# One-hot rows by scalar-operand instructions, a re-laid gate table, and GpSimd without elementwise work in the expert stages of a hybrid decoder layer

## The chip, the cores and the metric

The kernel runs on one core of a Trainium2 chip. The metric is the device time of the whole program in microseconds (us). The core has a matmul engine (PE, with its weight loads as PEld), a vector engine (DVE), a scalar engine (ACT), GpSimd (POOL) and a queue processor (SP) that issues most DMA transfers; sixteen DMA engines move the data. Each engine runs its own instructions in the order in which they stand.

## What is computed

A decoder layer over 512 positions of width 1024: RMS norm, one input projection, three groups of attention heads, an output projection with a residual, and then an expert retrieval. All of it is float32. The change lies in the last part:

```python
qry = (h @ w_q).reshape(B, S, PEER_HEADS, PEER_DKEY)
s1 = jnp.einsum('bshd,hkd->bshk', qry[..., :half], sub1)
s2 = jnp.einsum('bshd,hkd->bshk', qry[..., half:], sub2)
v1, i1 = lax.top_k(s1, PEER_TOPK)
v2, i2 = lax.top_k(s2, PEER_TOPK)
...
top_s, pos = lax.top_k(cand, PEER_TOPK)
expert = jnp.take_along_axis(cand_idx, pos, axis=-1)
gate = jax.nn.softmax(top_s, axis=-1)
...
def step(args):
    x_c, e_c, g_c = args
    a = jnp.einsum('cd,ced->ce', x_c, u[e_c])
    w = jax.nn.gelu(a, approximate=False) * g_c
    return jnp.einsum('ce,ced->cd', w, v[e_c])
```

Each position picks 8 x 16 = 128 of 16,384 experts (tables u and v, 64 MB each) and adds their gated outputs.

## The kernel before, in words

The 512 positions are four chunks of 128. Chunk 0 (GC) takes its experts by **gather**: for each of its 128 slots, GpSimd fetches one row of u per position by an indirect DMA (L475) and the vector engine forms the dot product (L482); then the same with v, where the vector engine adds even slots into one accumulator `ga` (L493) and GpSimd adds odd slots into a second one (L491) after the scalar engine has scaled the row (L490). Rows lie in four buffers, so GpSimd waits with a fetch until a row has been used.

The other three chunks (DC, TD = 384 positions) are computed **dense**: all 128 blocks of 128 experts are multiplied, and a gate table that is zero for experts not chosen picks out what counts. An fp32 product is made of three matmuls (L95 to L97) over a rounded part "hi" (scalar engine, L86) and a remainder "lo" (L87: a subtraction, 128x1024 for a block of u or v). `u_parts` (L514) loads a block of u and splits it; its remainder is GpSimd's. `a_block` (L521) multiplies it with the positions and applies the gelu (L527).

The stages as they lie in time:

- to about 300 us: attention and output projection, not touched;
- 315 to 562 us: expert queries, top-16 selections and `route` (L413), which turns the selections into expert numbers and gates, with the first blocks of u beside it. Some of `route`'s products (L442) stay on GpSimd in both kernels;
- 562 to 909 us, the **one-hot stage**: for each chunk `route` gives a tile `iT` with two key numbers and the gate of every slot. For four positions at a time the vector engine compares the key numbers with a ramp `iota` (L591, L592: 128x512 each), the second result is multiplied with the gate (half the times on the vector engine, L595; half on the scalar engine, L597), and PE multiplies the two (L600): 128 x 128 gates of one position. The scalar engine writes them to a tile `stage` (L601), and each 32 positions go out to HBM as a quarter of 2 MB (L602; `stage` has two buffers). Meanwhile the first 64 blocks of u run (NSP), and their results go to HBM (L607);
- 909 us to the end, the **table stage**: `w_block` (L628) runs 128 times. It reads its part of the gate table (L637, for four blocks at a time), loads a block of v (L641) and splits it (L86, L87), multiplies gelu and gate (L645), splits that, and issues 18 matmuls of 512 columns. 64 of these blocks also compute their u half here.

A scheduler sets the order of the instructions on each engine from its own forecast of the times, so an edit in one place moves instructions in others.

## Time and profile before

| | us |
|---|---|
| median of three runs | 1754.59 |
| lowest and highest | 1750.6, 1756.23 |
| span of the profiled execution, first to last instruction | 1749.3 |
| PE busy in it | 1592.6 |
| DVE busy | 1442.9 |
| POOL busy | 968.3 |

The profiled execution has no time of its own beside its span; the median lies 5.3 us above that span. The share of busy time is an average over stages that wait for different engines, so the profile is read by stage: which engine has no idle time there, and how long its instructions take against the shortest of the same form.

### The profile page before, as it was taken

The page shows a single profiled execution, that of the slowest core. Times are in us where ns is not written, and L with a number is a line of the kernel's source. Part 1 is how long each engine was busy: PE and PEld are TensorE (multiplying, and loading weights), DVE is VectorE, ACT ScalarE, POOL GpSimd, SP SyncE. Part 2 cuts the span into 40 slices and gives each one's busy share as a digit, 9 for nine tenths or more (in the row PEclk, how much of TensorE's full clock was granted, in tenths as well). Part 3 has the DMA queues.
Part 4 walks back from the last instruction along what each step waited for, and adds up shares of the span by engine and source line. Part 5 has one row for each costly group of instructions (what it writes and reads, how often), then busy time and mean ns, then how long its engine had stood idle before and what let it go on. Part 6 is the DMA issues. An engine that isn't in the chain of part 4 may idle for free.

```text
span 1749.3 us, 23459 instructions
## 1 busy us (share of the span) xinstructions
PE 1592.6 (91%) x8045; PEld 1397.1 (80%) x8045; DVE 1442.9 (82%) x2552; ACT 787.2 (45%) x1287; POOL 968.3 (55%) x531
## 2 busy tenths in 40 slices
PE   7999989997686878878999999999999999899997
PEld 6886667997686777778998888888888888788885
DVE  6556745899999999979956877877889978889896
ACT  6345633332332555667843333334444443444442
POOL 4220013363776675734465544456778867788774
PEclk9999999998888989889999999999999999999998
DMA  8302034132566566557699999998999999898894
GB/s 322 106 25 103 1 121 144 49 125 90 181 212 198 182 218 216 176 222 280 231 315 325 279 318 288 315 286 279 291 287 278 317 290 275 255 309 276 288 277 171
DMA packets 317463, 390.08 MB, mean 223 GB/s; under 512 B 214944, under 2 KB 240544, under 8 KB 314656
## 3 DMA queue, kind: packets, MB, share of 16 engines
q1 hardware_dynamic: 280480, 254.36, 46.0%
q0 software_dynamic: 36864, 134.23, 21.6%
q8 instruction: 63, 1.03, 0.2%
q14 instruction: 56, 0.46, 0.1%
HBM read 346.57 MB, written 41.94 MB: 222 GB/s over the span
## 4 chain that ended last, share of the span: by engine, by line
PE 49%; DVE 36%; issue 5%; DMA 5%; ACT 2%; SPq 2%; POOL 2%; DVEq 0%; ACTq 0%; POOLq 0%
PE s L96 7%; PE s L97 7%; PE s L95 6%; PE t L95 5%; PE t L97 5%; PE t L96 5%; DVE row L482 5%; DVE o L591 5%; DVE o L592 4%; PE o L96 3%; PE o L97 3%; PE o L95 3%; DVE eq L440 2%; PE o L330 2%; DVE og L595 2%
## 5 line engine op out<-in xcount | busy, mean ns | idle before, releaser
L87 POOL TENSOR_TENSOR yT<-flat,yT 128x1024 fp32r<-128x1024 f32 x128 | 346.6, 2709 | 216.4 <-ACT yT L86 208.7
L95 PE MATMUL t<-hT,yT 128*128 128x384 f32 x1024 | 351.4, 343 | 26.1 <-ACT ag L527 26.1
L97 PE MATMUL t<-hT,yT 128*128 128x384 f32 x1024 | 351.4, 343 | 2.4 <-POOL yT L87 2.4
L96 PE MATMUL t<-hT,yT 128*128 128x384 f32 x1024 | 350.3, 342 | 0.0
L87 DVE TENSOR_TENSOR yT<-vr,yT 128x1024 fp32r<-128x1024 f32 x128 | 209.5, 1637 | 54.7 <-ACT yT L86 51.5
L475 POOL DMA_INDIRECT row<-u,exp_g x128 | 161.7, 1263 | 124.0 <-DVE row L482 88.3
L95 PEld LDWEIGHTS t<-hT,yT 128*128 128x128 f32 x1024 | 197.0, 192 | 32.5 <-ACT ag L527 27.3
L96 PE MATMUL s<-yT,ws 128*128 128x512 f32 x512 | 206.7, 405 | 11.1 <-DVE yT L87 10.8
L482 DVE SCALAR_TENSOR_TENSOR row<-row,hg 128x1024 f32<-128x1024 f32 x128 | 189.2, 1482 | 24.0 <-DMA row<-u,exp_g 24.0
L97 PE MATMUL s<-yT,ws 128*128 128x512 f32 x512 | 201.4, 402 | 4.2 <-DVE ws L87 4.2
L475 POOL DMA_INDIRECT row<-v,exp_g x128 | 156.1, 1219 | 84.9 <-DVE ga L493 49.6
L86 ACT ACTIVATE ws<-w 128x384 fp32r<-128x384 f32 x128 | 67.1, 524 | 299.4 <-DVE w L645 118.7
L97 PEld LDWEIGHTS t<-hT,yT 128*128 128x128 f32 x1024 | 196.8, 192 | 5.7 <-POOL yT L87 3.0
L96 PEld LDWEIGHTS t<-hT,yT 128*128 128x128 f32 x1024 | 196.8, 192 | 4.5
L86 ACT ACTIVATE yT<-flat 128x1024 fp32r<-128x1024 f32 x128 | 135.4, 1058 | 144.2 <-issue 53.6
L491 POOL TENSOR_TENSOR ga<-ga,row 128x1024 f32<-128x1024 f32 x64 | 164.1, 2564 | 26.1 <-ACT row L490 25.4
L95 PE MATMUL s<-yT,ws 128*128 128x512 f32 x512 | 165.1, 399 | 7.8 <-ACT ws L86 7.8
L86 ACT ACTIVATE yT<-vr 128x1024 fp32r<-128x1024 f32 x128 | 134.2, 1048 | 57.4 <-DMA vr<-v 44.0
L600 PE MATMUL s<-og,o 128*128 128x128 f32 x768 | 109.7, 296 | 54.8 <-DVE og L595 38.4
L600 PEld LDWEIGHTS s<-og,o 128*128 128x128 f32 x768 | 103.1, 208 | 63.4 <-issue 39.6
L87 DVE TENSOR_TENSOR ws<-w,ws 128x384 fp32r<-128x384 f32 x128 | 119.8, 937 | 41.0 <-ACT ws L86 36.2
L493 DVE SCALAR_TENSOR_TENSOR ga<-row,gw,ga 128x1024 f32<-128x1024 f32 x64 | 143.2, 2238 | 6.6 <-DMA row<-v,exp_g 6.4
(268 smaller groups left out, 3249.2 us busy)
## 6 DMA issues: line engine op xcount, KB each, us to landing
flat<-uT SPq DMA_DIRECT2D x128, 512.0 KB
vr<-v SPq DMA_DIRECT2D x128, 512.0 KB
gd<-stage SPq DMA_DIRECT2D x12, 2048.0 KB
gt<-gd SPq DMA_DIRECT2D x384, 64.0 KB
ad<-ag SPq DMA_DIRECT2D x64, 192.0 KB
agr<-ad SPq DMA_DIRECT2D x64, 192.0 KB
wraw<-w_in SPq DMA_DIRECT2D x8, 1024.0 KB
flat<-w_q SPq DMA_DIRECT2D x16, 512.0 KB
```

The lines of the kernel that those rows point to most:

```text
L86: A.activation(hi, src, AF.Copy)
L87: return (e_lo or V).tensor_sub(lo, src, hi.bitcast(F32))
L95: T.matmul(o, ah, bh, start=start, stop=False)
L96: T.matmul(o, ah, bl, start=False, stop=False)
L97: T.matmul(o, al, bh, start=False, stop=stop)
L475: G.indirect_dma_start(out=row, out_offset=None, in_=table, in_offset=bass.IndirectOffsetOnAxis(ap=exp_g[:, s_:s_ + 1], axis=0))
L482: V.scalar_tensor_tensor(row, row, 1.0, hg, ALU.mult, ALU.mult, accum_out=av[:, s_:s_ + 1])
L491: G.tensor_add(ga[1], ga[1], row)
L493: V.scalar_tensor_tensor(ga[0], row, gw[:, s_:s_ + 1], ga[0], ALU.mult, ALU.add)
L591: V.tensor_tensor(o1, bc(iT[:, 0, :]), ib, ALU.is_equal)
L592: V.tensor_tensor(o2, bc(iT[:, 1, :]), ib, ALU.is_equal)
L600: T.matmul(gp[:, j, :], o1[:, j, :], og[:, j, :], start=True, stop=True)
```

## The change

- **One-hot**: per position, two instructions with a scalar operand for each partition. The first compares `iota` with the first key number; the second compares with the second key number and multiplies with the gate in the same instruction. 96 + 96 + 48 vector instructions of 128x512 and 192 scalar-engine instructions become 768 vector instructions of 128x128.
- **Gate table**: it is laid out in HBM by block, position row and position (`gd[NK, P, TD]`). A quarter is written in runs of 32 floats (128 bytes) instead of one run of 16 KB for each partition; a read of four blocks is one transfer with runs of 384 floats instead of twelve transfers that fill runs of 32 floats.
- **GpSimd**: the remainder of every block of u is computed on the vector engine, and all 128 slots of v are added by the vector engine into one accumulator. GpSimd keeps the indirect fetches and 20 products of `route`.

```diff
-    gd = [[dram.tile([P, NK, GT], F32, name=f"gd{c}_{q}") for q in range(P // GT)] for c in range(len(DC))]
+    gd = dram.tile([NK, P, TD], F32, name="gd")
...
             row = gather(v, s_)
-            if s_ % 2:
-                A.activation(row, row, AF.Copy, scale=gw[:, s_:s_ + 1])
-                G.tensor_add(ga[1], ga[1], row)
-            else:
-                V.scalar_tensor_tensor(ga[0], row, gw[:, s_:s_ + 1], ga[0], ALU.mult, ALU.add)
+            V.scalar_tensor_tensor(ga[0], row, gw[:, s_:s_ + 1], ga[0], ALU.mult, ALU.add)
...
-                    V.tensor_tensor(o1, bc(iT[:, 0, :]), ib, ALU.is_equal)
-                    V.tensor_tensor(o2, bc(iT[:, 1, :]), ib, ALU.is_equal)
-                    og = oh.tile([P, 4, NK], F32, tag="og", name="og", bufs=3)
-                    if OGD[t4 // 4 % len(OGD)] == "V":
-                        V.tensor_mul(og, o2, bc(iT[:, 2, :]))
-                    for j in range(0 if OGD[t4 // 4 % len(OGD)] == "V" else 4):
-                        A.activation(og[:, j, :], o2[:, j, :], AF.Copy, scale=iT[:, 2, t0 + j:t0 + j + 1])
+                    for j in range(4):
+                        i1, i2, gate = (iT[:, i, t0 + j:t0 + j + 1] for i in range(3))
+                        V.tensor_scalar(o1[:, j, :], iota, i1, None, ALU.is_equal)
+                        V.tensor_scalar(o2[:, j, :], iota, i2, gate, ALU.is_equal, ALU.mult)
...
-                        T.matmul(gp[:, j, :], o1[:, j, :], og[:, j, :], start=True, stop=True)
+                        T.matmul(gp[:, j, :], o1[:, j, :], o2[:, j, :], start=True, stop=True)
...
-                DMA.dma_start(gd[ci_][q], stage)
+                DMA.dma_start(gd[:, :, ci_ * P + q * GT:ci_ * P + (q + 1) * GT].rearrange("b p t -> p b t"), stage)
...
-                u_parts(loaded, loaded % 4, dict(G=G, V=V)[UL[loaded % len(UL)]])
+                u_parts(loaded, loaded % 4, V)
...
-                gt = vb.tile([P, NB, len(DC), P], F32, tag="gt", name="gt")
-                for ci_ in range(len(DC)):
-                    for q in range(P // GT):
-                        DMA.dma_start(gt[:, :, ci_, q * GT:(q + 1) * GT], gd[ci_][q][:, g0:g0 + NB, :])
+                gt = vb.tile([P, NB, TD], F32, tag="gt", name="gt")
+                DMA.dma_start(gt, gd[g0:g0 + NB].rearrange("b p t -> p b t"))
...
-                        u_parts(a, a % 2, G)
+                        u_parts(a, a % 2, V)
```

The edits move instructions on every engine. Three places show it (line numbers of the changed kernel are some 2 to 16 lower than those of the kernel before).

GpSimd near the end of the table stage, before: `yT<-flat` is the remainder of a block of u, `ga` the second accumulator, `row<-v` an indirect fetch.

```order
L475 DMA row<-v,exp_g 128x1024 x2
L491 TENSOR_TENSOR ga_1428<-ga_1428,row 128x1024
L87 TENSOR_TENSOR yT_1453<-flat,yT_1452 128x1024
L475 DMA row<-v,exp_g 128x1024 x2
L491 TENSOR_TENSOR ga_1428<-ga_1428,row 128x1024
L475 DMA row<-v,exp_g 128x1024 x2
L491 TENSOR_TENSOR ga_1428<-ga_1428,row 128x1024
```

GpSimd from the one-hot stage to the end, in the changed kernel:

```order
L440 TENSOR_TENSOR eq<-eq,ci 128x800 x2
L473 DMA row<-u,exp_g 128x1024 x7
L440 TENSOR_TENSOR eq<-eq,ci 128x800 x4
L473 DMA row<-u,exp_g 128x1024 x71
L473 DMA row<-v,exp_g 128x1024 x128
```

Between its fetches GpSimd has only `route`'s products left, and none after the 57th fetch of u.

The vector engine in the one-hot stage, before: the two comparisons and the gate product stand mixed with the dot products of the gathered rows.

```order
L592 TENSOR_TENSOR o_5220<-iT,iota 128x512
L482 SCALAR_TENSOR_TENSOR row,av<-row,hg 128x1024
L592 TENSOR_TENSOR o_5235<-iT,iota 128x512
L591 TENSOR_TENSOR o_5207<-iT,iota 128x512
L595 TENSOR_TENSOR og<-o_5208,iT 128x512
```

The same engine at the start of the one-hot stage in the changed kernel:

```order
L584 TENSOR_SCALAR o_4640<-iota,iT 128x128
L585 TENSOR_SCALAR o_4641<-iota,iT 128x128
L440 TENSOR_TENSOR eq<-eq,ci 128x800 x2
L445 TENSOR_TENSOR pe<-wv,wm 128x128
L85 TENSOR_TENSOR yT_1442<-flat,yT_1441 128x1024
L480 SCALAR_TENSOR_TENSOR row,av<-row,hg 128x1024
L85 TENSOR_TENSOR yT_1442<-flat,yT_1441 128x1024
L480 SCALAR_TENSOR_TENSOR row,av<-row,hg 128x1024
L85 TENSOR_TENSOR yT_1442<-flat,yT_1441 128x1024
L480 SCALAR_TENSOR_TENSOR row,av<-row,hg 128x1024
L584 TENSOR_SCALAR o_4656<-iota,iT 128x128
L585 TENSOR_SCALAR o_4657<-iota,iT 128x128
```

The remainders of u (L85) now stand in the vector engine's queue, each beside a dot product; the comparisons stand in runs, later for several quarters on end. Before the first `w` of the table stage the queue holds 71 remainders of u and 75 dot products, against 0 and 65 before.

The DMA queue of SP in the one-hot stage of the changed kernel: `gd<-stage` is a quarter of the gate table, `flat<-uT` a block of u, `ad<-ag` the result of a block.

```order
L590 DMA gd<-stage 128x128x32 x3
L510 DMA flat<-uT 128x1024 x3
L595 DMA ad_117<-ag 128x384
L595 DMA ad_118<-ag 128x384
L595 DMA ad_119<-ag 128x384
L510 DMA flat<-uT 128x1024
L595 DMA ad_120<-ag 128x384
L590 DMA gd<-stage 128x128x32 x4
```

Before, a quarter stood alone between loads of u; now three or four quarters follow one another, and the next loads of u stand behind them.

## Rows read from the trace of the kernel before

**Rows 1.** Stretches: busy us (instructions) of PE, PEld, DVE, ACT, POOL; clock, DMA, GB/s.

```profile
315.00:562.00 247.00, 196.54 (x1097) 191.30 (x1096) 246.90 (x1028) 78.54 (x115) 147.84 (x73) 0.90 0.44 146
562.00:909.00 347.00, 290.76 (x1807) 281.74 (x1806) 320.49 (x386) 211.04 (x377) 202.37 (x95) 0.93 0.64 225
909.00:1190.00 281.00, 279.95 (x1334) 243.22 (x1334) 215.00 (x259) 99.89 (x137) 138.91 (x87) 1.00 0.96 306
1190.00:1743.00 553.00, 530.05 (x2453) 452.70 (x2452) 472.52 (x322) 246.40 (x308) 411.56 (x227) 0.98 0.87 276
```

**Rows 2.** Groups of DVE, 315 to 909 us: busy us, mean ns of one.

```profile
L482 DVE SCALAR_TENSOR_TENSOR row<-row,hg 128x1024 f32<-128x1024 f32 x65 | 104.0, 1604 | 24.0 <-DMA row<-u,exp_g 24.0
L591 DVE TENSOR_TENSOR o<-iT,iota 128x512 f32<-128x512 f32 x96 | 96.7, 1022 | 0.0
L592 DVE TENSOR_TENSOR o<-iT,iota 128x512 f32<-128x512 f32 x96 | 89.5, 955 | 0.0
L440 DVE TENSOR_TENSOR eq<-wf,iota 128x800 f32<-128x800 f32 x32 | 41.7, 1320 | 0.0
L595 DVE TENSOR_TENSOR og<-o,iT 128x512 f32<-128x512 f32 x48 | 41.6, 868 | 0.0
```

**Rows 3.** Views by tile: duration ns min/median/max of three groups.

```profile
L482 DVE SCALAR_TENSOR_TENSOR row<-row,hg x128: 1194/1216/4674, 420.3 to 1185.5; 128x1024 f32<-128x1024 f32 x128
L493 DVE SCALAR_TENSOR_TENSOR ga<-row,gw,ga x64: 1271/1280/6280, 1191.0 to 1724.7; 128x1024 f32<-128x1024 f32 x64
L591 DVE TENSOR_TENSOR o<-iT,iota x96: 676/680/3277, 562.2 to 875.8; 128x512 f32<-128x512 f32 x96
```

**Rows 4.** Timelines of DVE and of POOL, 1694.6 to 1701.9: start us, us.

```profile
1694.67 0.56 DVE L87 TENSOR_TENSOR ws<-w,ws 128x384 fp32r<-128x384 f32 x1 [0.59 <-ACT ws L86]
1695.84 6.07 DVE L87 TENSOR_TENSOR yT<-vr,yT 128x1024 fp32r<-128x1024 f32 x1 [0.61 <-ACT yT L86]
...
1694.74 1.29 POOL L475 DMA_INDIRECT row<-v,exp_g  x1 [0.31 <-issue]
1696.06 2.40 POOL L87 TENSOR_TENSOR yT<-flat,yT 128x1024 fp32r<-128x1024 f32 x1
1698.41 2.41 POOL L491 TENSOR_TENSOR ga<-ga,row 128x1024 f32<-128x1024 f32 x1
```

**Rows 5.** Groups of POOL, 315 to 909 us.

```profile
L87 POOL TENSOR_TENSOR yT<-flat,yT 128x1024 fp32r<-128x1024 f32 x67 | 189.1, 2824 | 150.0 <-ACT yT L86 149.6
...
L442 POOL TENSOR_TENSOR eq<-eq,ci 128x800 f32<-128x800 f32 x20 | 45.5, 2283 | 51.8 <-DVE eq L440 50.4 <-PE s L600 1.3
L87 POOL TENSOR_TENSOR lo<-flat,hi 128x1024 fp32r<-128x1024 f32 x12 | 28.5, 2399 | 26.9 <-ACT hi L86 26.7 <-PE s L97 0.2
```

**Rows 6.** Timeline of DVE in the attention, 140.5 to 144.

```profile
140.60 0.28 DVE L313 TENSOR_SCALAR p<-p,den 128x128 f32<-128x128 f32 x1
140.80 0.68 DVE L304 CUSTOM_DVE_ANT_0 sb<-s,tab 128x512 f32<-128x512 f32 x1
...
142.15 0.35 DVE L313 TENSOR_SCALAR p<-p,den 128x256 f32<-128x256 f32 x1
```

**Rows 7.** A piece of the chain that ended last: start us, us, what.

```profile
780.53 1.80 DVE o L592 x3
```

**Rows 8.** DMA queues, 909 to 1743 us: packets, MB, share of 16 engines.

```profile
q1 hardware_dynamic: 233569, 138.36, 56.5%
q0 software_dynamic: 27321, 99.47, 33.4%
```

**Rows 9.** DMA queues and an issue, 562 to 909 us.

```profile
q1 hardware_dynamic: 19727, 55.02, 44.9%
q0 software_dynamic: 6231, 22.71, 18.4%
...
gd<-stage SPq DMA_DIRECT2D x12, 2048.0 KB
```

**Rows 10.** Issues of the whole run, from the page: KB each.

```profile
gt<-gd SPq DMA_DIRECT2D x384, 64.0 KB
```

More of the change, by code (lines that the diff above doesn't have):

```diff
@@ L45 @@
 SCB = 4
-UL = "GGGG"
 EM = 4
-OGD = "AV"
 GR = 1.0
@@ L531, in layer_kernel @@
         mix_out([GC] + DC, yT, rg, hT, "l")
-        for t in ga:
-            G.memset(t, 0.0)
+        G.memset(ga[0], 0.0)
         rp = ctx.enter_context(tile_pool(name="rp", bufs=1, side="right"))
@@ L644, in w_block @@
             w = vb.tile([P, TD], F32, tag="w", name="w")
-            V.tensor_mul(w.rearrange("p (c t) -> p c t", t=P), ag.rearrange("p (c t) -> p c t", t=P),
-                         gt[:, b % NB, :, :])
+            V.tensor_mul(w, ag, gt[:, b % NB, :])
             ws = [vb.tile([P, TD], F32R, tag=f"ws{i}", name=f"ws{i}") for i in range(2)]
@@ L673, in layer_kernel @@
             if c == GC:
-                for t in ga:
-                    V.tensor_add(xr, xr, t)
+                V.tensor_add(xr, xr, ga[0])
             else:
```

2 lines of the change are left out of this document (removed).

## The prediction

> **What bounds the kernel now.** I read the busy times by stretch first, to find the engine without idle time in each stage, then the groups of that engine with their mean against their shortest time, and then the timeline around one long instruction to see what stretches it. Three things are to be seen.
>
> In routing and one-hot stage (315 to 909 us, 594 us in all) the vector engine sets the pace: it is busy 247 of 247 us and then 320 of 347 us, while PE is busy 197 and 291 us [rows 1]. Much of that is not work. The comparisons of 128x512 take 0.68 us at the median, yet 1.02, 0.96 and 0.87 us in the mean of the three groups; the dot product takes 1.216 us at the median and 1.604 us in the mean of this stretch [rows 2, 3].
>
> The stretching has a visible cause. One remainder of v, which otherwise takes about as long as the dot product, takes 6.07 us; it ends when two GpSimd elementwise instructions of 2.40 and 2.41 us end [rows 4]. A remainder of `w` just before it takes its ordinary 0.56 us with an indirect fetch of 1.29 us running beside it [rows 4]. So the vector engine is held up by GpSimd's arithmetic and not by its fetches.
>
> In the table stage (909 us to the end) PE sets the pace. Before 1190 us it starts 1334 matmuls in 281 us, 4.75 per us, and is idle 1 us. After 1190 us, when GpSimd also adds rows of v, it starts 2453 in 553 us, 4.44 per us [rows 1]. At the earlier pace those would have taken 517 us, so 36 us are lost there. GpSimd is busy 49% of the time in the first part and 74% in the second, the DMA engines 96% and 87% [rows 1]; the loss goes with GpSimd and not with DMA.
>
> **Routing and one-hot stage, term by term.** *Stretch removed.* Mean less undisturbed time, by group: 96 x 0.342 = 33 us (L591), 96 x 0.275 = 26 (L592), 48 x 0.188 = 9 (L595), 65 x 0.388 = 25 (dot products), and 32 x 0.34 = 11 for the 128x800 comparison, whose undisturbed 0.98 us is 0.680 us and 288 more elements at the step from 512 to 1024 [rows 2, 3]. That is 104 us. The smaller groups of the same view (candidate sums, casts, copies, not shown) add about 55 us by the same subtraction, an estimate. Of GpSimd's 263 us of arithmetic in this stretch the 189 us of remainders of u go, while 45.5 us of `route`'s products and 28.5 us of query-weight remainders stay [rows 5]. I take 72% of 159 us: **115 us** off. Bounds: 75 us (72% of the 104 alone) and 159 us.
>
> *Remainders of u added.* By the order of the changed program 71 of them stand before the first `w`. Instructions in a row start sooner than one ends: three comparisons take 1.80 us, 0.60 each against 0.68 in duration [rows 3, 7]. With 0.08 us off the 1.216 us of an instruction of this size, one costs 1.14 us: **81 us** on. Ten dot products more than before stand there too (75 against 65): **11 us** on, taken out of the next stage.
>
> *One-hot.* Before: 240 vector instructions at 0.60 us, 144 us. After: 768 of 128x128. The nearest row is a multiplication by one value per partition, of that size: 0.28 us long, the next instruction 0.20 us after its start [rows 6]. The second instruction has a second such operand. One costs about 0.06 us (1.280 against 1.216 us in two otherwise like instructions [rows 3]); whether two cost twice that no row shows, so 0.20 to 0.26 us. That gives 384 x 0.20 + 384 x (0.20 to 0.26) = 154 to 177 us; in the middle **21 us** on. The 192 gate products on the scalar engine go, but that engine is busy 211 of 347 us [rows 1] and nothing waits at its end, so they are worth nothing.
>
> *Gate table writes.* The trace has no write of 128 bytes. The fetches on the software queue give the price of large packets: 33.4% of 834 us on 16 engines for 99.5 MB is 44.8 us of one engine per MB. On the hardware queue 114 MB of the 138.4 MB are large, 5110 us at that price; the other 2430 us belong to about 370 of the 384 small reads of 64 KB, 189,000 packets of 128 bytes: 12.8 ns each [rows 8, 10]. If a write costs the same, the table takes 196,608 x 12.8 ns / 16 = 157 us of all engines, where it takes 25.2 MB x 44.8 / 16 = 70 us now. The DMA engines work 63.3% of 347 us there, 220 us [rows 9]; after the change 307 of 347 us. That fits, but tightly, and SP's queue holds loads of u behind three or four quarters: I put **10 us** of waiting (0 to 30) on it.
>
> The runs of comparisons may also hold up the fetches. A fetch of 1.29 us ran beside a two-input vector instruction of 0.56 us, and neither was long [rows 4]; no row shows a fetch beside an instruction with one tensor operand, as the new comparisons are. The page "SBUF — State Buffer" of the Trainium skill (the "DVE blocks DMA" trap) says that GpSimd can't write the descriptors of its fetches while the vector engine runs a copy-like instruction in a mode that takes both ports. By that rule the four row buffers would be filled only after each long run of comparisons: four fetches of 1.3 us, for about three runs, an estimate of 15 us, which would raise the 10 us of waiting to 25. No row here shows whether it holds.
>
> Sum of this stage: -115 + 81 + 11 + 21 + 10 = **+8 us**. The vector engine exchanges waiting for work here, and the stage stays as long as it was.
>
> **Table stage, term by term.** GpSimd's arithmetic ends entirely, so the pace of the first part should hold throughout: of the 36 us I leave 6 us for the start and the last blocks, **30 us** off (bounds 0 and 36). 71 matmuls of u blocks have moved ahead of the first `w` by the order of the program; at 4.75 per us that would be 15 us, and since they are shorter than the 512-column ones I take **12 us** off. Ahead they are hidden: PE was idle 107 of 594 us there [rows 1].
>
> Does the vector engine become the bound? Its work here: 128 blocks x (1.14 + 0.48 + 0.48) = 269 us (0.48 us is the 0.56 us of an instruction of 128x384 [rows 4] less the same 0.08), 53 dot products 60 us, 128 additions of v at 1.20 us 154 us, 57 remainders of u 65 us: 548 us of about 800, 69%. Before, it was busy 687 of 834 us, 82% [rows 1]. The remainder of u is a new stop on the way to PE, but 2.4 us on GpSimd [rows 4] become 1.14 us. The reads of the gate table in long runs save 24 MB x (100 - 44.8) = 1340 us of one engine (12.8 ns for 128 bytes are 100 us per MB), 84 us of all 16; since PE lost nothing at a share of 96%, I count them at nothing.
>
> **Sum.** +8 - 30 - 12 = -34 us. The profiled span becomes 1715 us, and the median, 5.3 us above it, about **1720 us**.
>
> **The rivals.** *A: small writes cost more than small reads.* The DMA engines have room in the one-hot stage up to (347 - 149) / 157 x 12.8 = 16 ns for a write, 149 us being the other traffic (220 - 70). Each ns beyond costs 196,608 / 16 = 12.3 us, since `stage` has two buffers and the vector engine then waits for them. At 19 ns the gain of 34 us is gone. A write that is carried out as a read and a write, 25.6 ns, gives 1720 + 9.5 x 12.3 = **1837 us**. For it: 128 bytes scattered at a distance of 192 KB, where the small reads took four neighbours at a time; the vector engine makes a quarter in 64 x 0.21 = 13 us in the long runs, so nothing waits in between. Against it: the reads too moved 128-byte pieces, and at only 12.8 ns.
>
> The page "DMA: Bandwidth & Descriptors" of the Trainium skill (Specifications) says that below 512 bytes a DMA engine reads, modifies and writes. By that rule, rival A holds; the small reads of this trace, at 10 bytes per ns against 22 for large packets, show that small packets are dear but not that a write costs twice.
>
> *B: the comparison runs at half the rate of the row I took.* From 128 to 256 elements that row grows by 0.07 us [rows 6], half of what a 128x512 comparison takes for as many (0.60 us less its fixed part). A comparison that takes one element per cycle costs 0.07 us more, 768 x 0.07 = 54 us: **1774 us**. For it: no comparison of this form is in the trace. Against: the instruction kind is the same.
>
> *C: no difference.* The 36 us in the table stage belong to the landing of gathered rows behind which the in-order vector engine waits, and not to GpSimd: then 1720 + 30 = **1750 us**. For it: all 128 additions of v now stand in the queue that feeds PE. Against: the part without additions, at a higher DMA share, loses nothing. That GpSimd still has 20 products of `route` falls here too: it would leave more of the stretch than I took.
>
> **How the numbers follow.** Forecast 0.47, with a range of its own of 1688 to 1748 us (stretch 75 to 159, second operand, waiting 0 to 30 us); A 0.28, B 0.10, C 0.15. Faster by over 0.3% means below 1749 us, about what a measurement of this kernel tells from no change: the forecast and almost half of C with a little of the rest, 0.55. Within 0.3%, up to 1760 us: most of the rest of C and the mild end of A, 0.09. Slower: most of A, B, 0.36. The range runs from 1688 us to 1815 us: the half of A with the dearest writes (0.14) and 0.06 at the low end are left out.
>
> **What would show it.** The comparisons of 128x128 at about 0.20 us from start to start; remainders of u on the vector engine near 1.22 us long, and no instruction of 128x1024 over 2 us after 600 us; the first `w` near 915 us; over 4.7 matmuls per us to the end. Wrong: 128-byte writes above 16 ns with the vector engine idle on `stage` buffers (A), comparisons 0.26 us apart or more (B), PE still below 4.5 matmuls per us with the vector engine waiting for `row` (C).

## The result

The changed kernel takes 1705.24 us in the median (1703.33 to 1709.62), against 1755.41 us before in the same comparison (1750.6 to 1756.6). The ratio is 0.9743 with a 95% interval of 0.9705 to 0.9781: 50 us or 2.6% faster. 1720 us were forecast, with a range of 1688 to 1815 us. The profiled execution spans 1707.8 us, against 1749.3 us, and was itself the slowest of the four (1709.62 us).

### The profile page after: what moved, and what is told of

Its sections match the earlier page's. It is cut to its first block, busy times and chain, and to the rows that moved or that the text cites. A ratio compares the mean times of both kernels' runs of the same rounds, so it can differ in the third digit from the quotient of the medians.

```text
span 1707.8 us, 23283 instructions
## 1 busy us (share of the span) xinstructions
PE 1621.6 (95%) x8045; PEld 1406.2 (82%) x8045; DVE 1318.7 (77%) x3271; ACT 672.1 (39%) x1031; POOL 464.6 (27%) x338
## 5 line engine op out<-in xcount | busy, mean ns | idle before, releaser
L473 POOL DMA_INDIRECT row<-u,exp_g x128 | 166.4, 1300 | 455.0 <-DVE row L480 338.6
L85 DVE TENSOR_TENSOR yT<-flat,yT 128x1024 fp32r<-128x1024 f32 x128 | 163.7, 1280 | 69.3 <-ACT yT L84 64.1
L85 DVE TENSOR_TENSOR yT<-vr,yT 128x1024 fp32r<-128x1024 f32 x128 | 156.4, 1223 | 71.8 <-ACT yT L84 71.5
L94 PE MATMUL s<-yT,ws 128*128 128x512 f32 x512 | 202.7, 396 | 0.0
L95 PE MATMUL s<-yT,ws 128*128 128x512 f32 x512 | 193.3, 396 | 0.0
L93 PE MATMUL s<-yT,ws 128*128 128x512 f32 x512 | 167.3, 396 | 0.0
L487 DVE SCALAR_TENSOR_TENSOR ga<-row,gw,ga 128x1024 f32<-128x1024 f32 x128 | 163.8, 1279 | 0.9
L480 DVE SCALAR_TENSOR_TENSOR row<-row,hg 128x1024 f32<-128x1024 f32 x128 | 159.0, 1251 | 0.0
L588 PE MATMUL s<-o,o 128*128 128x128 f32 x768 | 153.2, 310 | 3.1
L588 PEld LDWEIGHTS s<-o,o 128*128 128x128 f32 x768 | 118.5, 195 | 36.5 <-DVE o L585 18.2
L85 DVE TENSOR_TENSOR ws<-w,ws 128x384 fp32r<-128x384 f32 x128 | 70.5, 556 | 93.9 <-ACT ws L84 91.0
L585 DVE TENSOR_SCALAR o<-iota,iT 128x128 f32<-128x128 f32 x384 | 129.6, 338 | 0.0
```

The lines of the kernel that those rows point to most:

```text
L85: return (e_lo or V).tensor_sub(lo, src, hi.bitcast(F32))
L93: T.matmul(o, ah, bh, start=start, stop=False)
L94: T.matmul(o, ah, bl, start=False, stop=False)
L95: T.matmul(o, al, bh, start=False, stop=stop)
L473: G.indirect_dma_start(out=row, out_offset=None, in_=table, in_offset=bass.IndirectOffsetOnAxis(ap=exp_g[:, s_:s_ + 1], axis=0))
L480: V.scalar_tensor_tensor(row, row, 1.0, hg, ALU.mult, ALU.mult, accum_out=av[:, s_:s_ + 1])
```

## Profile after the change

The stretches of the changed kernel, as in [rows 1] (busy us and instructions of PE, PEld, DVE, ACT, POOL; clock, DMA share, GB/s). The first `w` of the table stage now starts at 912 us.

```profile
315.00:562.00 247.00, 236.16 (x1361) 230.99 (x1360) 245.17 (x1027) 93.83 (x136) 94.14 (x59) 0.98 0.60 197
562.00:912.00 350.00, 302.02 (x1625) 264.29 (x1624) 316.90 (x1004) 152.57 (x170) 82.46 (x50) 0.93 1.04 212
912.00:1190.00 278.00, 276.02 (x1301) 239.82 (x1302) 217.57 (x293) 98.56 (x136) 99.94 (x83) 0.99 0.94 340
1190.00:1698.00 508.00, 508.00 (x2402) 440.14 (x2402) 349.74 (x388) 176.50 (x240) 121.45 (x97) 1.00 0.75 266
```

The last row is the gain: PE is busy 508 of 508 us and starts 4.73 matmuls per us, where it started 4.44 with 23 us of idle time [rows 1]. Idle time is not all of it: while busy, PE started 4.63 per us before (2453 in 530 us), and the clock granted to it was 0.98 of full speed before and is 1.00 now. The DMA share of 1.04 in the second row is the sum of the packets' times; above 1 it can't be the engines' occupancy alone, so packets overlap. The vector engine has fallen from 472 of 553 to 350 of 508 us there, although it now adds every row of v. The first two rows together are as long as before: the vector engine is still without idle time up to 562 us and busy 317 of 350 us after it.

The costliest groups of the vector engine, 315 to 909 us (instructions; busy us, mean ns of one; idle time before them), to be read beside [rows 2]:

```profile
L585 DVE TENSOR_SCALAR o<-iota,iT 128x128 f32<-128x128 f32 x384 | 129.6, 338 | 0.0
L584 DVE TENSOR_SCALAR o<-iota,iT 128x128 f32<-128x128 f32 x384 | 105.4, 275 | 5.0 <-PE s L588 5.0
L85 DVE TENSOR_TENSOR yT<-flat,yT 128x1024 fp32r<-128x1024 f32 x71 | 94.0, 1325 | 24.1 <-ACT yT L84 24.1
L480 DVE SCALAR_TENSOR_TENSOR row<-row,hg 128x1024 f32<-128x1024 f32 x73 | 92.5, 1275 | 0.0
L438 DVE TENSOR_TENSOR eq<-wf,iota 128x800 f32<-128x800 f32 x32 | 31.9, 1019 | 0.1
```

A dot product now takes 1.28 us in the mean instead of 1.60, the comparison of `route` 1.02 instead of 1.32 [rows 2]. The stretching has nearly gone; the 71 remainders of u and the larger one-hot have taken its place. The waits are others too: 24.0 us before dot products, for fetched rows [rows 2], have become 0.0, and 24.1 us before remainders of u are new; there the scalar engine waits for the load of the block.

Views by tile (duration ns min/median/max, first and last start): the changed kernel, then the first product `w` of the kernel before.

```profile
L631 DVE TENSOR_TENSOR w<-ag,gt x64: 544/551/559, 912.4 to 1677.7; 128x384 f32<-128x384 f32 x64
L487 DVE SCALAR_TENSOR_TENSOR ga<-row,gw,ga x128: 1272/1279/1289, 1099.4 to 1515.3; 128x1024 f32<-128x1024 f32 x128
```

```profile
L645 DVE TENSOR_TENSOR w<-ag,gt x64: 544/1890/5194, 908.6 to 1714.4; 128x384 f32<-128x384 f32 x64
```

The longest addition of a row of v takes 1.289 us, where it took 6.28 us [rows 3]; the longest `w` 0.559 us instead of 5.194. From the first `w` to the last instruction pass 795.4 us (1707.8 - 912.4), against 840.7 us (1749.3 - 908.6). This second number is the key to all runs below: **the time is the start of the first `w` plus what follows it**, so each run is told by these two.

## The experiments

The twelve further kernels were measured in three sets of four, each on one chip beside the kernel before; the ratios refer to that. Its median was 1749.46 us beside the two layouts, GpSimd's part alone and the one-hot alone; 1749.05 us beside fewer dot products, GpSimd's two tasks and the old one-hot; 1754.39 us beside the last two steps with the old one-hot, `route` on the vector engine and the layout alone. Where a comparison crosses these sets, the ratios decide and the differences in us are good to a few us. The two right-hand times are those of the one profiled execution of each kernel. "Dot products ahead" are those that the order of the program puts before the first `w`.

| run | median us | ratio, 95% interval | first w at | from there to the end | dot products ahead |
|---|---|---|---|---|---|
| changed kernel | 1705.24 | 0.9743 (0.9705 to 0.9781) | 912.4 | 795.4 | 75 |
| runs of 16 KB | 1711.82 | 0.9802 (0.9759 to 0.9845) | 907.7 | 799.3 | 84 |
| runs of 512 bytes | 1704.21 | 0.9751 (0.9712 to 0.9789) | 908.3 | 796.1 | 82 |
| GpSimd's part alone | 1743.25 | 0.9965 (0.9946 to 0.9985) | 945.0 | 797.6 | 128 |
| one-hot alone | 1782.5 | 1.021 (1.0169 to 1.025) | 962.5 | 815.5 | 84 |
| layout alone | 1783.41 | 1.0184 (1.0141 to 1.0226) | 916.7 | 865.4 | 62 |
| fewer dot products | 1660.61 | 0.9489 (0.9461 to 0.9518) | 858.5 | 796.2 | 49 |
| GpSimd adds odd rows of v | 1719.37 | 0.9829 (0.9799 to 0.986) | 905.8 | 806.9 | 75 |
| GpSimd's early remainders | 1749.45 | 1.001 (0.9989 to 1.003) | 952.9 | 793.5 | 66 |
| old one-hot | 1678.91 | 0.9595 (0.9566 to 0.9624) | 880.9 | 795.7 | 87 |
| old one-hot, 61 dot products | 1641.83 | 0.9365 (0.932 to 0.9411) | 845.2 | 796.3 | 61 |
| gates on the scalar engine | 1619.29 | 0.9237 (0.9201 to 0.9272) | 826.0 | 796.0 | 43 |
| route on the vector engine | 1669.36 | 0.9527 (0.9489 to 0.9564) | 870.2 | 796.5 | 55 |

### The table's layout: is the wait for small writes worth anything?

In the changed kernel PE is busy 9.08 of the 27 us before the first `w`, and the loads of u that it wants stand on SP's queue behind a quarter's write. I took that for the price of the small writes, and tried two other layouts. Runs of 16 KB, the layout before:

```diff
-    gd = dram.tile([NK, P, TD], F32, name="gd")
+    gd = [[dram.tile([P, NK, GT], F32, name=f"gd{c}_{q}") for q in range(P // GT)] for c in range(len(DC))]
```

> The changed kernel with one part undone: the gate table in HBM is laid out as before (writes of 16 KB runs, reads of 128 bytes); the rest as changed. Theory W (the small writes are what is left to gain): in the changed kernel PE stands still for about 18 us between 885 and 912 us, behind loads of u that stand behind the last quarter's write. With large writes that stop goes: about 1690 us, first product w near 895 us, and the table stage keeps its 796 us, since PE didn't notice 128-byte reads before. Rival L (the long reads gave the table stage its pace): the stage falls back to 4.5 matmuls per us, some 35 us are lost there, and the total is 1720 us or more.

Runs of 512 bytes (written) and 6 KB (read):

```diff
-    gd = dram.tile([NK, P, TD], F32, name="gd")
+    gd = dram.tile([NK // NB, P, TD // GT, NB * GT], F32, name="gd")
...
-                DMA.dma_start(gd[:, :, ci_ * P + q * GT:ci_ * P + (q + 1) * GT].rearrange("b p t -> p b t"), stage)
+                DMA.dma_start(gd[:, :, ci_ * (P // GT) + q, :].rearrange("g p n -> p g n"),
+                              stage.rearrange("p (g b) t -> p g (b t)", b=NB))
```

> The changed kernel with a third layout of the gate table, by group of four blocks, position row, quarter, block and position: writes in runs of 512 bytes, reads in runs of 6 KB. The computation is the same. Theory W: 49,152 packets in place of 196,608; at the 65 ns that a 1536-byte packet takes as upper bound a write of 512 bytes takes under 30 ns, so a quarter lands in about half the time and the stop before the table stage falls from 18 us to under 8 us: 1690 to 1697 us. Rival Q (it is the order of the queue, four quarters in a row ahead of the loads, and not the size of the runs): the stop stays, 1705 us. Rival L gives 1690 us too, so this run and the one with 16 KB runs tell W from L together.

Neither theory held: 1711.82 and 1704.21 us, the first `w` only 4 to 5 us sooner, and no loss in the table stage. The writes themselves behaved as thought. Queues and an issue, 562 to 912 us (packets, MB, share of 16 engines; KB each, median us to landing), for the changed kernel and then for runs of 512 bytes:

```profile
q1 hardware_dynamic: 207578, 52.57, 85.2%
q0 software_dynamic: 5829, 21.19, 17.9%
...
gd<-stage SPq DMA_DIRECT2D x12, 2048.0 KB, 16.5
```

```profile
q1 hardware_dynamic: 59902, 53.08, 45.7%
q0 software_dynamic: 7208, 26.26, 21.3%
...
gd<-stage SPq DMA_DIRECT2D x12, 2048.0 KB, 7.9
```

85.2% of 350 us on 16 engines is 4771 us. With 44.8 us per MB for the other 27.4 MB, as in the prediction, 3544 us are left for 196,608 writes: 18.0 ns each, as a packet's time while others overlap it. In the second run 2559 us less 27.9 x 44.8 leave 1309 us for 49,152 writes of 512 bytes, 26.6 ns each. A quarter lands in half the time. Yet PE still stands before the first `w`; here are the stretches from 884 to 912 us of the run with 16 KB and of the run with 512 bytes (columns as above):

```profile
884.00:912.00 28.00, 1.99 (x9) 1.43 (x10) 14.84 (x29) 3.89 (x6) 14.05 (x10) 0.58 0.91 296
```

```profile
884.00:912.00 28.00, 8.83 (x38) 6.63 (x38) 19.24 (x51) 7.60 (x10) 11.46 (x8) 0.67 0.74 265
```

In both runs PE has no block of u left by then: its last matmuls are the one-hot's, and it then waits for work that hangs on the first `w`. The vector engine's waiting before the first `w` did fall, from 33 to 18 and 15 us; for loads of u it is now 0 and 5 us, where it was 24. Its dot products and remainders of u up to the first `w`, with runs of 16 KB and of 512 bytes:

```profile
L480 DVE SCALAR_TENSOR_TENSOR row<-row,hg 128x1024 f32<-128x1024 f32 x84 | 109.0, 1306 | 16.6 <-DMA row<-u,exp_g 16.5
L85 DVE TENSOR_TENSOR yT<-flat,yT 128x1024 fp32r<-128x1024 f32 x71 | 96.7, 1363 | 0.0
```

```profile
L480 DVE SCALAR_TENSOR_TENSOR row<-row,hg 128x1024 f32<-128x1024 f32 x82 | 105.0, 1289 | 8.6 <-DMA row<-u,exp_g 8.5
L85 DVE TENSOR_TENSOR yT<-flat,yT 128x1024 fp32r<-128x1024 f32 x71 | 98.5, 1388 | 5.0 <-ACT yT L84 5.0
```

But the scheduler had put 9 and 7 more dot products there, 11 and 8 us at 1.2 us each. So what the writes cost was given back as work that could have waited. That became the new theory: the vector engine's queue ahead of the first `w` sets the time, and the dot products in it are ballast.

### GpSimd's part alone

```diff
-                u_parts(loaded, loaded % 4, dict(G=G, V=V)[UL[loaded % len(UL)]])
+                u_parts(loaded, loaded % 4, V)
...
-            if s_ % 2:
-                A.activation(row, row, AF.Copy, scale=gw[:, s_:s_ + 1])
-                G.tensor_add(ga[1], ga[1], row)
-            else:
-                V.scalar_tensor_tensor(ga[0], row, gw[:, s_:s_ + 1], ga[0], ALU.mult, ALU.add)
+            V.scalar_tensor_tensor(ga[0], row, gw[:, s_:s_ + 1], ga[0], ALU.mult, ALU.add)
```

(and the other remainders of u likewise).

> The kernel before with one part of the change alone: the remainders of u and the additions of all 128 rows of v on the vector engine; one-hot and gate table as before. The scheduler now puts all 128 dot products ahead of the first w (75 in the changed kernel). Theory G (the gain is GpSimd's arithmetic alone): against the changed kernel's 912 us the first w comes 53 x 1.14 = 60 us later for the dot products, 30 us sooner for the cheaper one-hot of before (144 against 174 us), and some 16 us sooner for the large writes: 927 us; then 796 us of table stage: 1723 us, with 4.7 matmuls per us or more. Rival F (the new one-hot form brings the gain, GpSimd little): the 81 us of remainders and 72 us of dot products come on top of 909 us, with the stretch as before: 1850 us or more.

1743.25 us: between the theories, 20 us above mine. The table stage is 797.6 us, so GpSimd's arithmetic alone was what PE lost there. The first `w` comes at 945 us where I expected 927. The term that I had left out is 12 additions of rows of v, which the scheduler also put ahead of the first `w` (the last line below): 15 us. The rest came out near: the dot products cost 62 us more than in the changed kernel (60 expected), the old one-hot 24 less (30), the waiting fell by 14 (16), and this execution began its first top-16 some 5 us sooner. Groups of the vector engine from 315 to 945 us:

```profile
L482 DVE SCALAR_TENSOR_TENSOR row<-row,hg 128x1024 f32<-128x1024 f32 x128 | 161.4, 1263 | 4.3 <-DMA row<-u,exp_g 4.2
L87 DVE TENSOR_TENSOR yT<-flat,yT 128x1024 fp32r<-128x1024 f32 x71 | 94.0, 1324 | 0.0
L586 DVE TENSOR_TENSOR o<-iT,iota 128x512 f32<-128x512 f32 x96 | 69.4, 732 | 0.0
L587 DVE TENSOR_TENSOR o<-iT,iota 128x512 f32<-128x512 f32 x96 | 65.7, 696 | 0.0
L590 DVE TENSOR_TENSOR og<-o,iT 128x512 f32<-128x512 f32 x48 | 32.6, 680 | 0.0
...
L489 DVE SCALAR_TENSOR_TENSOR ga<-row,gw,ga 128x1024 f32<-128x1024 f32 x12 | 15.4, 1283 | 10.7 <-DMA row<-v,exp_g 10.4
```

The old one-hot, at 0.73, 0.70 and 0.68 us in the mean, shows its price without GpSimd's arithmetic. And all 128 dot products stand ahead of the first `w`, 161 us.

### The one-hot alone

The one-hot part of the diff, with nothing else:

```diff
-                    V.tensor_tensor(o1, bc(iT[:, 0, :]), ib, ALU.is_equal)
-                    V.tensor_tensor(o2, bc(iT[:, 1, :]), ib, ALU.is_equal)
+                        V.tensor_scalar(o1[:, j, :], iota, i1, None, ALU.is_equal)
+                        V.tensor_scalar(o2[:, j, :], iota, i2, gate, ALU.is_equal, ALU.mult)
```

> The kernel before with one part of the change alone: the one-hot by scalar-operand instructions (384 at 0.20 us and 384 at 0.26 us from start to start in the changed kernel's trace); GpSimd and the gate table as before. 84 dot products stand ahead of the first w, against 65. Theory G: GpSimd's arithmetic in that stage is the same, so the stretch is the same; 30 us for the one-hot and 22 us for dot products come on top: first w near 960 us, total about 1800 us less what the table stage gains by dot products that it no longer has (it waits for PE, so nothing). Rival S (instructions with one tensor operand are not stretched beside GpSimd): the stretch of 33 + 26 + 9 us of the old one-hot groups goes, first w near 890 us, total about 1740 us. The two forms' mean durations say which: near 0.28 and 0.34 us (S) or well above (G).

1782.5 us, 2.1% slower: the first `w` comes at 962.5 us as theory G said, and the table stage shortens from 840.7 to 815.5 us, which I had not thought of (19 dot products have left it; whether that is the reason was not tested). The groups, 315 to 962 us:

```profile
L592 DVE TENSOR_SCALAR o<-iota,iT 128x128 f32<-128x128 f32 x384 | 173.2, 451 | 0.0
L591 DVE TENSOR_SCALAR o<-iota,iT 128x128 f32<-128x128 f32 x384 | 165.4, 431 | 0.0
```

0.45 and 0.43 us, against 0.34 and 0.28 in the changed kernel: rival S is wrong, the new form is stretched beside GpSimd too, and more than the old one.

### Fewer dot products ahead of the first w

```diff
-GR = 1.0
+GR = 0.5
```

on the kernel with runs of 512 bytes.

> The kernel with 512-byte runs, and one constant changed: half as many steps of the gather chunk are tied to the 64 early blocks (GR 0.5 in place of 1.0), so that 49 dot products stand ahead of the first w and not 82; the other 33 stand among the blocks of the table stage. The computation is the same. Theory V (the vector engine's queue ahead of the first w sets that time; what the large runs freed was filled with dot products by the scheduler): 33 x 1.2 = 40 us less for the vector engine, so the first w near 870 us, the table stage 796 us or little more (the vector engine was busy there 69 to 79%), total 1665 to 1675 us. Rival P (PE or the loads take over at once, since PE is idle only some 70 us between 315 and 912): less than 15 us gained, 1690 us or more. Rival E (rows of v come too late: the last addition stands behind the 113th w, where it was the 96th): the end is held up, 1700 us.

```profile
L631 DVE TENSOR_TENSOR w<-ag,gt x64: 549/552/559, 858.5 to 1624.3; 128x384 f32<-128x384 f32 x64
```

1660.61 us. The first `w` starts at 858.5 us, 50 us sooner than with 82 dot products: 39 us for the 33 of them, 7 us because the first top-16 of this execution began that much sooner, 4 us of smaller differences, and the table stage takes 796.2 us with the 33 in it. The theory held, and the rivals didn't: PE had room before, and the later rows of v didn't hold up the end.

### GpSimd's two tasks, one at a time

In the changed kernel, the odd rows of v go back to GpSimd:

```diff
-            V.scalar_tensor_tensor(ga[0], row, gw[:, s_:s_ + 1], ga[0], ALU.mult, ALU.add)
+            if s_ % 2:
+                A.activation(row, row, AF.Copy, scale=gw[:, s_:s_ + 1])
+                G.tensor_add(ga[1], ga[1], row)
+            else:
+                V.scalar_tensor_tensor(ga[0], row, gw[:, s_:s_ + 1], ga[0], ALU.mult, ALU.add)
```

> The changed kernel with one part undone: GpSimd adds the odd rows of v again (64 additions after a scaling on the scalar engine); nothing else. Theory G (GpSimd's arithmetic holds the vector engine up, and PE through it): the first w stays near 912 us, and of the 36 us that the kernel before lost behind 1190 us about half comes back, since it had remainders of u there besides: 1717 to 1728 us, with instructions of the vector engine of over 2 us in that stretch. Rival C (the loss came from the landing of gathered rows): the vector engine has 77 us less work, and the time stays at 1705 us or falls.

1719.37 us, as theory G said. From 1190 us on, and the remainders of v:

```profile
1190.00:1702.00 512.00, 508.03 (x2393) 437.72 (x2392) 387.46 (x336) 229.65 (x290) 260.67 (x148) 1.00 0.75 265
```

```profile
L85 DVE TENSOR_TENSOR yT<-vr,yT x128: 1209/1219/3941, 909.1 to 1700.3; 128x1024 fp32r<-128x1024 f32 x128
```

The vector engine has 52 instructions fewer in this stretch (336 against 388) and is busy longer, 387 us against 350; remainders of up to 3.94 us are back, where the longest of the changed kernel takes 1.23 us. From the first `w` to the end it takes 806.9 instead of 795.4 us: 64 additions on GpSimd cost 11.5 us there. Rival C of the prediction falls. (The median stands 14 us above the changed kernel's. The first `w` of the profiled execution came 6.6 us sooner than there with the same order ahead of it; 5.7 us of that are there at the first top-16 already, a difference between executions.)

The early remainders of u go back to GpSimd:

```diff
-                u_parts(loaded, loaded % 4, V)
+                u_parts(loaded, loaded % 4, G)
```

> The changed kernel with one part undone: the remainders of the 64 early blocks of u are GpSimd's again; 66 dot products stand ahead of the first w, against 75. Theory X (in that stage the vector engine merely changes waiting for work): it saves 65 remainders at 1.25 us, 81 us, and 9 dot products, 11 us, and is stretched again. The run with the one-hot alone showed 155 us of stretch for 263 us of GpSimd's arithmetic in that stage; 160 us of remainders would give some 95 to 110 us: first w between 912 and 935 us, total 1705 to 1730 us. Rival D (remainders on the vector engine are a bad exchange): the total falls below 1695 us.

1749.45 us, 19 us beyond my upper end: this one edit gives back all of the change's gain. The groups, 315 to 952 us:

```profile
L584 DVE TENSOR_SCALAR o<-iota,iT 128x128 f32<-128x128 f32 x384 | 168.6, 439 | 3.5 <-PE s L588 3.4
L585 DVE TENSOR_SCALAR o<-iota,iT 128x128 f32<-128x128 f32 x384 | 168.4, 439 | 0.0
```

The vector engine is rid of 65 remainders and 9 dot products (92 us), and the first `w` comes 40 us later. 159 us of GpSimd's arithmetic stretched it by some 140 us, 94 of them in the one-hot. I had expected 95 to 110 us, from the ratio of the run with the one-hot alone.

### The old one-hot in the new surroundings

The kernel with runs of 512 bytes, with the one-hot of before and GR 0.5:

```diff
-                    for j in range(4):
-                        i1, i2, gate = (iT[:, i, t0 + j:t0 + j + 1] for i in range(3))
-                        V.tensor_scalar(o1[:, j, :], iota, i1, None, ALU.is_equal)
-                        V.tensor_scalar(o2[:, j, :], iota, i2, gate, ALU.is_equal, ALU.mult)
+                    V.tensor_tensor(o1, bc(iT[:, 0, :]), ib, ALU.is_equal)
+                    V.tensor_tensor(o2, bc(iT[:, 1, :]), ib, ALU.is_equal)
```

(with the gate products `og` behind them).

> The kernel with 512-byte runs, with the one-hot of before (comparisons and gate products of 128x512, half of the products on the scalar engine), and GR 0.5 so that about as many dot products stand ahead of the first w as with the new form (87 against 82). So it differs from the kernel with 512-byte runs by the one-hot's form. Theory H (the new form costs the vector engine more, 175 us against 151 us where GpSimd doesn't disturb it, and gains nothing by itself): 24 us saved, 6 us for five more dot products: about 18 us less, first w near 890 us, 1686 us. Rival N (the new form gains elsewhere, by the scalar engine's 192 products or the shorter way to PE): 1704 us or more.

1678.91 us, against 1704.21 us with the new form and five dot products fewer ahead. Theory H holds, with 25 us where 18 were expected: with about as many dot products ahead the new form is a loss. Of this, 23 us are the one-hot (153 against 176 us); another 8 came off the remainders of u, and the dot products took 3 more. Two further steps go down the same way, fewer dot products ahead, and then all gate products on the scalar engine:

```diff
-GR = 0.5
+GR = 0.25
```

> The kernel of the run with the old one-hot and 512-byte runs, with GR 0.25: 61 dot products stand ahead of the first w, against 87; the last addition of a row of v stands behind the 106th w. The computation is the same. Theory V (the vector engine's queue sets the first w): 26 x 1.17 = 30 us less, first w near 851 us, total about 1649 us. Rival P (PE has run out of room): less than 10 us gained, 1669 us or more.

```diff
-OGD = "AV"
+OGD = "A"
```

> As the run with the old one-hot and 61 dot products, but all gate products on the scalar engine (384 instead of 192), none on the vector engine; 43 dot products stand ahead of the first w. The computation is the same. Theory V: against 61 dot products the vector engine has 29 us of gate products and 18 x 1.17 = 21 us of dot products less: first w near 801 us, total 1600 us. Rival P (PE, idle some 70 us between 315 and 880 in the run with 87 dot products, or the scalar engine, with some 60 us more than 193 of 288, takes over before that): 1615 to 1640 us.

1641.83 and 1619.29 us, the fastest here: 7.6% below the kernel before, 5% below the changed one. The first `w` of the two runs:

```profile
L638 DVE TENSOR_TENSOR w<-ag,gt x64: 549/551/559, 845.2 to 1611.4; 128x384 f32<-128x384 f32 x64
```

```profile
L638 DVE TENSOR_TENSOR w<-ag,gt x64: 548/551/560, 826.0 to 1591.9; 128x384 f32<-128x384 f32 x64
```

26 dot products fewer brought 36 us, a little more than the 30 expected. The last step brought 19 us of the 50 that the vector engine was relieved of, as rival P said. The stretch from 562 to 800 us shows who sets the pace now:

```profile
562.00:800.00 238.00, 232.41 (x1549) 226.30 (x1548) 210.62 (x308) 226.42 (x506) 53.56 (x34) 1.00 0.78 257
```

PE is busy 232 and the scalar engine 226 of 238 us, the vector engine 211. Up to the first `w` the vector engine now waits 39 us instead of 18, 33 of them for the scalar engine.

### The last of GpSimd's arithmetic

On the kernel with fewer dot products (1660.61 us):

```diff
-            (V if q < EM and nq == PH else G).tensor_mul(eq, eq, ci[:, q, None, :].to_broadcast([P, TK, NCAND]))
+            V.tensor_mul(eq, eq, ci[:, q, None, :].to_broadcast([P, TK, NCAND]))
```

> The kernel with 512-byte runs, the new one-hot and GR 0.5 (1660 us), with the last elementwise work of GpSimd in the routing, 20 products of route (54 us in all on GpSimd), on the vector engine too; 55 dot products stand ahead of the first w, against 49. The computation is the same. Theory X (GpSimd's arithmetic stretches the vector engine by about 0.7 us for each us, as the run with the early remainders on GpSimd showed: 140 us for 155 us, and the one with the one-hot alone): 18 us for 20 products at 0.9 us and 7 us for six dot products on, 38 us of stretch off: 13 us less, 1648 us. Rival D (moving the last of it is no gain, since these products lay beside work that isn't stretched): 25 us more, 1685 us.

1669.36 us, the first `w` at 870.2 instead of 858.5 us, 2 us of that by a later first top-16. The two ratios, 0.9527 and 0.9489, have intervals that overlap, so that it is slower at all is not shown; the 13 us that theory X promised did not come. The products added 18 us, the six dot products 7, and the stretch fell by some 19 us, not 38. What these 54 us on GpSimd stood beside was not followed up. The price per us of GpSimd's arithmetic isn't a constant: 0.35 here, about 0.9 for the early remainders.

### The layout alone

The layout's part of the diff, on the kernel before:

```diff
-                DMA.dma_start(gd[ci_][q], stage)
+                DMA.dma_start(gd[:, :, ci_ * P + q * GT:ci_ * P + (q + 1) * GT].rearrange("b p t -> p b t"), stage)
```

> The kernel before with one part of the change alone: the gate table's layout (writes of 128 bytes, reads in long runs); the rest as before. 62 dot products stand ahead of the first w, against 65. Theory W (a write of 128 bytes took 18 ns in the changed kernel, 196,608 of them 221 us of all 16 engines in place of some 70): the vector engine waits some 10 to 20 us more ahead of the first w, and the table stage gains nothing: 1755 to 1770 us. Rival L (the long reads are worth something in the table stage, whose DMA share was 87 to 96%): 1735 us or less.

1783.41 us, 1.8% slower, more than theory W gave. The first `w` comes at 916.7 us, 8 us later, about as expected. The other 25 us were lost behind it, which no theory said:

```profile
1190.00:1743.00 553.00, 518.55 (x2363) 441.99 (x2362) 446.35 (x302) 237.09 (x297) 398.22 (x217) 0.96 0.76 269
```

PE starts 2363 matmuls where it started 2453 [rows 1], although the DMA share has fallen from 0.87 to 0.76. Part of the loss is PE's clock, granted at 0.96 of full speed where it was 0.98: PE stands still for 34 us of this stretch instead of 23, and its clock falls to the lower level, 1.2 instead of 2.4 GHz, eight times instead of four, mostly after such an idle spell. What differs on GpSimd is the order: the last row of v is added behind the 106th `w` and not the 127th, so that its arithmetic lies closer together. That this is the cause was not tested, and the run with the one-hot alone speaks against it: there the last row is added behind the 114th `w`, and the table stage is shorter than before, not longer. The cause of these 25 us stays open.

## Why the prediction held

**What bounds each stage.** Right in both. The table stage depends on GpSimd's arithmetic: without any, it took 793.5 to 799.3 us in ten runs of three one-hot and three layout variants, with any 806.9 to 865.4. With the same arithmetic it still varies, from 815.5 to 865.4 us in the three runs with both tasks on GpSimd, and the runs don't show why. One reading needs a correction: the remainder of 6.07 us [rows 4] does not end with the second GpSimd instruction but 1.1 us after it, as if it had been held through both and then done in about its usual time.

**The routing and one-hot stage, term by term.** For each instruction of the vector engine in order I counted the time by which it moves the engine's end of work on, from the first top-16 to the first `w`, in us (idle with the wait directly before the first `w`):

| kind (instructions before, after) | before | changed | GpSimd's part alone |
|---|---|---|---|
| selections, sums, casts (994, 994) | 194 | 165 | 166 |
| comparisons and products of `route` (44, 44) | 56 | 41 | 40 |
| dot products (65, 75; 128 in the last) | 100 | 91 | 153 |
| remainders of u (0, 71) | 0 | 89 | 88 |
| one-hot (240, 768; 240 in the last) | 213 | 175 | 151 |
| gate products of chunk 0 (4, 4) and, in the last, 12 additions to `ga` | 4 | 1 | 16 |
| idle | 27 | 33 | 19 |
| whole time | 594 | 596 | 633 |

- *Stretch removed:* forecast 115 us (75 to 159), measured 131: 29 + 15 + 3 from the first, second and sixth line, 62 from the one-hot (213 against the 151 that the same instructions take nearly undisturbed, last column), 22 from the dot products (100 against 65 x 1.195, with 1.195 = 153 / 128).
- *Remainders of u:* forecast 81, measured 89, 1.25 us each instead of 1.14.
- *Dot products moved ahead:* forecast 11, measured 13 (91 - 78).
- *One-hot:* forecast 21, measured 24 (175 - 151). Which end of the range held, rows of the changed kernel settle: the second instruction of a position starts 0.20 us behind the first and the next position 0.26 us behind the second, so a second operand costs another 0.06 us. Rival B, the half rate, falls.

```profile
868.28 0.34 DVE L585 TENSOR_SCALAR o<-iota,iT 128x128 f32<-128x128 f32 x1
868.54 0.28 DVE L584 TENSOR_SCALAR o<-iota,iT 128x128 f32<-128x128 f32 x1
868.74 0.34 DVE L585 TENSOR_SCALAR o<-iota,iT 128x128 f32<-128x128 f32 x1
```

- *Waiting:* forecast 10, measured 6.5 (33.1 - 26.6), and that this is near is luck. The prediction added new waits to the old ones. In fact the 24 us for fetched rows [rows 2] went, which it had not thought of, and 33 us of new waits came: 24 for loads of u, of which 14.5 in one piece just before the first `w`, 5 for PE at the one-hot and 4 for a product of `route`. With larger writes the waiting is 15 and 18 us less, so the small writes cost about that much, as far as kernels with another order on the vector engine can show it. Why the old waits went was not tested.

The sum was +8, measured +2 for the whole and 4 us for the start of the first `w` (912.4 against 908.6). These terms are large and nearly cancel. The run that puts the early remainders back shows what the exchange of stretch for remainders is worth: the first `w` comes 40 us later.

**The table stage.** Forecast -42 us, measured -45 us (795.4 - 840.7). From 909 to 1743 us 3787 matmuls started, 797 us at 4.75 per us, so 37 us were lost; after, 3703 from 912 to 1698 us, 780 us at that pace, 6 us lost. So 31 us came from the stalls, idle time and slower clock together (forecast 30) and 18 us from matmuls that had moved ahead (84 records fewer; 71 had been counted, at 12 us), less 3 us that lie outside the two stretches.

**Span and median.** The span was to be 1715 us and is 1707.8. The 5.3 us that I laid on top for the median did not come: this profiled execution was the slowest of its four, where that of before was below the median. That accounts for the other half of the 15 us by which the forecast was high.

**The signs.** Two of them were missed narrowly. Three instructions of 128x1024 took over 2 us after 600 us (2.67, 2.78 and 2.75 us, at 622, 625 and 687 us), each beside products of `route` on GpSimd. From 912 to 1190 us PE started 4.68 matmuls per us and not 4.7; to 1698 us the mean is 4.71.

**Rival A.** A 128-byte write took 18.0 ns, above the 16 ns that I gave as the point of decision, and below twice the 12.8 ns of a read [rows 8, 10]. The page "DMA: Bandwidth & Descriptors" of the Trainium skill (Specifications) has transfers under 512 bytes carried out as read, modify and write; the trace agrees that such writes are dear per byte (18.0 ns for 128 bytes, 26.6 for 512), and shows no doubling against a read. At 12.3 us for each ns beyond 16, rival A would have cost 25 us of waiting; the 15 to 18 us above are most of that, so its mechanism was at work, and the forecast was saved by the old waits that went. Taking the small writes away gains next to nothing for another reason: the work ahead of the first `w` isn't fixed. In the kernels with larger writes the scheduler put more dot products there.

**What the prediction did not see.** It counted the ten dot products moved ahead as a small term and took the order as given. The runs show that this is the largest lever: the one-hot alone and the layout alone lose 33 and 29 us, GpSimd's part alone gains 6, and all three together gain 50. The run with 16 KB runs differs from the one with GpSimd's part alone by the one-hot only: 84 dot products and no addition of v stand ahead of the first `w`, and not 128 and 12, and it comes 37 us sooner (907.7 against 945.0), although the one-hot takes 24 us longer. The one-hot, dearer by itself, brought the first `w` forward by what it kept out of the queue. Why the scheduler's forecast then put fewer there was not looked into.

## What to carry to other kernels

Before pricing an edit, find the one instruction whose start sets the rest of the time, and read what stands ahead of it on its engine that isn't needed by it: here each dot product held back was worth 1.3 to 1.4 us (43 us for 33, 36 for 26), while a transfer made twice as quick moved it by 4 to 5 us. An engine that waits in a stage bounded by a second engine's arithmetic is better given that arithmetic itself, if it costs it less than the stretch. Parts of a change that a scheduler sees must be tried together and apart, since each moves the filler of the others.

## What the hardware showed unexpectedly

Short instructions of the vector engine are lengthened beside GpSimd's arithmetic by as much as long ones. In the run with the one-hot alone the comparison of 0.275 us takes up to 2.93 us, about as long as a GpSimd instruction lasts, and so does the old one of 0.68 us (up to 3.28 us [rows 3]). From the first to the last one-hot instruction GpSimd has 132 us of arithmetic in both kernels, but 61 of the 768 short ones are over 0.1 us longer than their median, against 34 of the 240 long ones: 98 us of stretch (274 against 175 us) where the old form had 62.

Some fetches are long too. In the run with fewer dot products one takes 12.81 us; it starts within a long stretch of comparisons, with three other instructions in its middle, and ends when that does. GpSimd, and the vector engine at the start and at the end of the fetch (start us, us):

```profile
668.19 12.81 POOL L473 DMA_INDIRECT row<-u,exp_g  x1 [0.30 <-DVE o L585]
```

```profile
668.04 0.40 DVE L585 TENSOR_SCALAR o<-iota,iT 128x128 f32<-128x128 f32 x1
668.30 0.34 DVE L584 TENSOR_SCALAR o<-iota,iT 128x128 f32<-128x128 f32 x1
...
680.28 0.35 DVE L584 TENSOR_SCALAR o<-iota,iT 128x128 f32<-128x128 f32 x1
680.47 0.41 DVE L585 TENSOR_SCALAR o<-iota,iT 128x128 f32<-128x128 f32 x1
680.73 1.94 DVE L441 TENSOR_REDUCE ex<-eq 128x16 f32<-128x800 f32 x2
```

This row looks like what the "DVE blocks DMA" trap of the Trainium skill's page "SBUF — State Buffer" describes, but no run shows that it is that. Most fetches beside the same comparisons took 1.0 us, and a fetch of the changed kernel is long with no comparison beside it, only dot products, remainders of u and the instructions of `route`:

```profile
771.68 6.02 POOL L473 DMA_INDIRECT row<-u,exp_g  x1 [62.52 <-DVE row L480]
```

Both long fetches start 2 to 3 us after SP issues a quarter of the gate table (at 666.2 and 769.0 us). So the quarter's write is a rival cause, and the runs don't tell the two apart. It cost no time that shows: in the changed kernel the vector engine sat idle 0.0 us before its dot products in that stage, since rows lay ready in the other buffers.
